# Gated delta rule in a decoder layer: k and q kept in two parts for their products, q's sums of squares by block transposes

## Chip, core and metric

The kernel runs on one core of a Trainium2 chip. A core has a matrix engine (TensorE, here PE; PEld is its weight load), a vector engine (DVE), a scalar engine (ACT), GpSimd (POOL) and a sync engine (SP), each with its own instruction queue that it works through in order; they meet at semaphores. The metric is the device time of one execution in microseconds (us), lower is better.

## What is computed

One layer of a hybrid decoder for 256 tokens and a width of 2048, in float32. After an RMS norm one projection gives q, k, v, z, two small gates, a pooling input and two channel gates. q and k (16 heads of 128) go through a causal convolution of 4 taps and SiLU, are scaled to unit length, and enter a gated delta rule in chunks. What the change touches is this:

```python
qkv = silu(causal_dwconv(concatenate([q, k, v]), conv_qkv_w))
q = l2norm(q) * HEAD_DIM ** -0.5          # l2norm: x * rsqrt(sum(x*x) + EPS)
k = l2norm(k)
lmat = where(strict, einsum('nid,njd->nij', k * beta, k) * decay, 0)
u, w = triangular_solve(lmat + eye, [v * beta, k * beta * exp(g)])
attn_intra = einsum('nid,njd->nij', q, k) * decay
...
o = rmsnorm(o, gdn_norm_w) * silu(z)
```

The mixer's output is merged with a causal pooling branch, projected and added to x; then follow a gated MLP (width 5632) with a convolution of 3 taps and a final norm. Each output must match the float32 reference closely, so that plain reduced-precision products aren't enough.

## The kernel before

Each large GEMM is split: a weight tile `raw` of 256 rows by 512 columns (a chunk) is cast by ACT into a high part `whi` in the format float32r (L131), and DVE makes the low part `wlo` = raw - whi (L139). The activations are held in two such parts as well. `gemm_a` (L156 on) then makes three products a step, high by high, low by high and high by low (L169 to L171), with 512 columns each; a chunk has 12 of them. `weights()` keeps the parts two chunks ahead (`AHEAD = 2`) in three buffers each. `gemm_b` (L193, L194), for the FFN, makes a product of 512 and one of 256 columns a step.

The mixer runs in four groups of four heads (loop at L790). A group's GEMMs are, in order, k, q, v, pooling input, a gate, the pooling weights, z and a gate. A result is scaled out of PSUM by ACT into the one buffer `ev` (`evict`, L526). `conv_silu` (L566) turns it with PE, makes the four taps on ACT and DVE (L577, L580), the tanh on ACT (L583), and writes the SiLU to one half of the tile `kq` (L584); it is called when the next GEMM starts its second chunk (the list `later`). v goes to DRAM (`vrow`) and comes back as shifted copies `mv` (L550), which DVE weighs and adds (L557, L558).

The rest of the delta rule is the generator `gdn` (L586): `side()` in `gemm_a` advances it by one step after each half chunk, from v's GEMM on. Its steps are: decay factors `dec0`, `dec1`; for each head two full float32 products of k with [k q] (L631, L633) into two PSUM tiles; from their diagonal the sums of squares of k (L636); the scaled and decayed tiles `ga0`, `ga1` (L646, L650); diagonal blocks sent through DRAM to a layout (`lb`) in which DVE solves eight problems at once (L676, L678); the inverse T put together from blocks (L697 to L739); products with v (`w1`, `w2`, L745 to L757); the output products `po` (L763 to L766); the squares of q on ACT (L760) and their sums as eight full float32 products of a 128x128 block of squares with a column of ones (L771); and the output's norm (L772 to L786). After its last GEMM a group drains what is left of the generator (`gated`).

The order of each engine's queue isn't written out by hand, except for the first GEMM: the framework plans it at build time from the order of the code and a simulated timeline (`schedule_with_timeline_sim=True`), and sets the semaphores. Tiles of the same tag share its buffers (`bufs`, 1 in this pool unless stated), and a new tile of a tag waits until all that used the older one are done.

Of the kernel before, what the change touches and what calls it, by code (L numbers as in the profile page):

```python
# [13 lines left out]
P = 128  # L14
S = 256
# [18 lines left out]
def kernel(  # L34
# [36 lines left out]
    def pg(shape=(P, 512)):  # L71
        return psg.tile(list(shape), F32, tag="g", name=nm("psg"))
# [133 lines left out]
    def turned(src):  # L206

        out = []
        for f2 in range(2):
            pt = pg([P, 2, S])  # L210
            for ff in range(2):
                f = 2 * f2 + ff
                for t in range(2):
                    nc.tensor.transpose(pt[:, ff, t * P : (t + 1) * P], src[:, t, f * P : (f + 1) * P], ident)
            out.append(pt)
        return out
# [23 lines left out]
    mix = tc.tile_pool(name="mix", bufs=1)  # L240
    mp = mix.__enter__()

    nmrows = mp.tile([KD, P], F32, tag="w1", name="nmrows")
    nc.scalar.dma_start(nmrows, norm_mix_w[0].rearrange("(r p) -> r p", p=P))
    x0 = []
    for c in range(4):
# [174 lines left out]
    nc.vector.tensor_tensor(id2, ident[:64, 0:32], ident[:64, 32:64], op=ALU.add)  # L421


    pba = pg([P, 2, S])
    for c in range(2):
        hi, lo = weights()
        for kk in range(8):
            k = 8 * c + kk
            mm(pba, hi[:, kk, :], xhl[:, k], start=(k == 0), stop=(k == KD - 1))
    bat = mp.tile([64, 2, S], F32, tag="u", name="bat")  # L430
    nc.vector.tensor_copy(bat, pba[:64])
    pbt = pg([P, 2, 32])
    for t in range(2):
# [131 lines left out]

    def conv_silu(e, kind, g, dst):  # L566

        pts = turned(e)
        y = mp.tile([P, 4, S], F32, tag="cy", bufs=2, name=nm("cy"))
        for f in range(4):  # L570
            r = kind * 16 + 4 * g + f
            gs = pts[f // 2][:, f % 2, :]

            def w(j):
                return cqw[:, j * 48 + r : j * 48 + r + 1]

            nc.scalar.activation(y[:, f, :], gs, AF.Copy, scale=w(3))  # L577
            for j in (2, 1, 0):
                s = 3 - j
                nc.vector.scalar_tensor_tensor(y[:, f, s:], gs[:, : S - s], w(j), y[:, f, s:],  # L580
                                               op0=ALU.mult, op1=ALU.add)
        th = mp.tile([P, 4, S], F32, tag="th", name=nm("th"))
        nc.scalar.activation(th, y, AF.Tanh)  # L583
        nc.vector.scalar_tensor_tensor(dst, th, 1.0, y, op0=ALU.add, op1=ALU.mult)  # L584

    def gdn(g, kq, vt, conv, res):  # L586

        ga0 = mp.tile([P, 4, 512], F32, tag="ga0", name=nm("ga0"))
        ga1 = mp.tile([P, 4, 256], F32, tag="ga1", name=nm("ga1"))
# [2 lines left out]
        sj = mp.tile([P, 2, 4], F32, tag="sj", name=nm("sj"))  # L592
        dec0 = mp.tile([P, 4, S], F32, tag="dec0", name=nm("dec0"))
        dec1 = mp.tile([P, 4, P], F32, tag="dec1", name=nm("dec1"))
        for hp in range(2):

            h0 = 2 * hp
            rx = []
            for part, gp in (("h", ghi.bitcast(F32)), ("l", glo)):
                r0 = mp.tile([P, 2, P], F32R, tag="r0" + part, name=nm("r0"))  # L600
                r1 = mp.tile([P, 2, P], F32R, tag="r1" + part, name=nm("r1"))
                for i in range(2):
                    hh = 4 * g + h0 + i
                    nc.vector.tensor_scalar(r0[:, i], tri, gp[:, 0, hh : hh + 1], None, op0=ALU.mult)
                    nc.vector.tensor_scalar(r1[:, i], tri, gp[:, 1, hh : hh + 1], None, op0=ALU.mult)
                rx.append((r0, r1))
            yield
            pd0 = pg([P, 2, P])
            pdx = pg([P, 2, P])
            pd1 = pg([P, 2, P])  # L610
            for n, (r0, r1) in enumerate(rx):
                mm(pd0, lowr, r0, start=(n == 0), stop=(n == 1))
                mm(pd1, lowr, r1, start=(n == 0), stop=(n == 1))
            for n, (r0, r1) in enumerate(rx):
                mm(pdx, onesr, r1, start=(n == 0), stop=(n == 1))
            nc.scalar.activation(dec0[:, h0 : h0 + 2, 0:P], pd0, AF.Exp)
            nc.scalar.activation(dec1[:, h0 : h0 + 2, :], pd1, AF.Exp)
            for i in range(2):
                hh = 4 * g + h0 + i
                nc.scalar.activation(dec0[:, h0 + i, P:S], pdx[:, i, :], AF.Exp, bias=tail[:, hh : hh + 1])  # L620
            for d in (dec0[:, h0 : h0 + 2, 0:P], dec1[:, h0 : h0 + 2, :]):
                nc.gpsimd.affine_select(d, d, pattern=[[0, 2], [1, P]], compare_op=ALU.is_ge, fill=0.0, base=0,
                                        channel_multiplier=-1)
            yield
        for hp in range(2):
# [2 lines left out]
            grams = []  # L628
            for h in (h0, h0 + 1):
                pg0 = pg()  # L630
                mm(pg0, kq[:, h, 0, 0:P], kq[:, h, :, :], start=True, stop=True)  # L631
                pg1 = pg([P, 2, P])
                mm(pg1, kq[:, h, 0, P:S], kq[:, h, :, P:S], start=True, stop=True)  # L633
                jk = mp.tile([P, P], F32, tag="jk", name=nm("jk"))
                for t, src in ((0, pg0[:, 0:P]), (1, pg1[:, 0, :])):
                    nc.vector.tensor_tensor_reduce(jk, src, ident, scale=1.0, scalar=0.0, op0=ALU.mult,  # L636
                                                   op1=ALU.add, accum_out=ssk[:, t, h : h + 1])
                grams.append((pg0, pg1))
                yield
# [50 lines left out]
        for h in range(4):  # L690
            for t in range(2):
                nc.scalar.activation(vt[:, t, h, :], vt[:, t, h, :], AF.Copy, scale=nk[:, t, h : h + 1])
        for _ in range(WAIT - 3):
            yield
        for r in range(NR):
            rs = slice(B0 * r, B0 * (r + 1))
            nc.vector.transpose(Ta[rs, :, rs], TTa[rs, :, rs])  # L697
# [40 lines left out]
                mm(px[lo, t, i, :], U[hp][up, t, i, :], TT[hp][up, t, i, up], start=True, stop=True)  # L738
            nc.vector.tensor_scalar(TT[hp][lo, :, :, up], px[lo], -1.0, None, op0=ALU.mult)  # L739
        yield  # L740
        w1 = mp.tile([P, 4, P], F32, tag="w1", name=nm("w1"))
        w2 = mp.tile([P, 4, P], F32, tag="w2", name=nm("w2"))
        pw = pg([P, 4, P])
        for h in range(4):
            mm(pw[:, h, :], TT[h // 2][:, 0, h % 2, :], vt[:, 0, h, :], start=True, stop=True)  # L745
# [9 lines left out]
            mm(pw[:, h, :], TT[h // 2][:, 1, h % 2, :], vt[:, 1, h, :], start=True, stop=True)  # L755
        nc.scalar.copy(w2, pw)
        yield  # L757

        q2 = kq[:, :, 1, :]
        nc.scalar.activation(q2, q2, AF.Square)  # L760
        po = [pg([P, 4, P]) for t in range(2)]
        for h in range(4):
            mm(po[0][:, h, :], ga0[:, h, 256:384], w1[:, h, :], start=True, stop=True)  # L763
# [1 line left out]
            mm(po[1][:, h, :], ga0[:, h, 384:512], w1[:, h, :], start=True, stop=False)  # L765
            mm(po[1][:, h, :], ga1[:, h, P : 2 * P], w2[:, h, :], start=False, stop=True)  # L766
        yield
        pn = pg([P, 2, 4])
        for t in range(2):
            for h in range(4):  # L770
                mm(pn[:, t, h : h + 1], q2[:, h, t * P : (t + 1) * P], ones[:, 0:1], start=True, stop=True)  # L771
        ro = mp.tile([P, 2, 4], F32, tag="ro", name=nm("ro"))  # L772
        so = mp.tile([P, 2, 4], F32, tag="so", name=nm("so"))
        for t in range(2):
# [1 line left out]
            nc.scalar.activation(o2, po[t], AF.Square, scale=float(P) ** -0.5)  # L776
            nc.vector.tensor_reduce(so[:, t, :], o2, axis=mybir.AxisListType.X, op=ALU.add)
        yield
        nc.vector.tensor_scalar(ro, pn, EPS * P, EPS * EPS * P, op0=ALU.mult, op1=ALU.add)
        nc.vector.tensor_tensor(ro, ro, so, op=ALU.add)  # L780
        nc.gpsimd.tensor_tensor(ro, ro, epsx[:, 0:1].unsqueeze(2).to_broadcast([P, 2, 4]), op=ALU.pow)
        for t in range(2):
# [5 lines left out]
        res.append(on)  # L788

    for g in range(4):  # L790
        kq = mp.tile([P, 4, 2, S], F32, tag="kq", bufs=1, name=nm("kq"))
        for kind, dst in ((1, kq[:, :, 0, :]), (0, kq[:, :, 1, :])):
            ps = ps_k0 if kind == 1 and g == 0 else gemm_a(xh, xl, KD)
            e = evict(ps)
            later.append(lambda e=e, kind=kind, g=g, dst=dst: conv_silu(e, kind, g, dst))
# [1 line left out]
        vt = mp.tile([P, 2, 4, P], F32, tag="vt", name=nm("vt"))  # L797
        vt2 = vt.rearrange("p t h d -> p t (h d)")
        res = []
        later.append(lambda g=g, kq=kq, vt=vt, res=res: side_work.__setitem__(0, gdn(g, kq, vt, v_conv(g, vt), res)))  # L800
        v_taps(g)
        e = evict(gemm_a(xh, xl, KD), rsh)
        nc.sync.dma_start(vrow[g, SH : SH + S, :].rearrange("(t p) d -> p t d", p=P), e)
# [239 lines left out]
```

## Time and profile before

| what | value |
|---|---|
| median of 3 runs | 1576.41 us (1576.08 to 1577.27) |
| the profiled execution's own time | 1577.52 us |
| its span | 1575.6 us |
| mean granted PE clock | 0.999 |
| bytes moved by DMA | 304 MB, mean 193 GB/s |
| mixer's four groups | from some 40 to 780 us |

The profile shows one execution. A row with "x8" stands for eight instructions merged in order of time; times in it are start, length. Lengths of PE's products overlap, so that their cost is read from start to start. A full float32 product shows as two records. In rows of groups the columns after the bar are busy time and mean length in ns, then the engine's idle time before them and what ended it.

### The profile page before, as it was taken

To read this page: it belongs to the slowest core of one execution; us is meant where nothing else is said; L and a number is where in the kernel's file an instruction comes from. 1 tells how busy PE (TensorE), PEld (TensorE's weight loads), DVE (VectorE), ACT (ScalarE), POOL (GpSimd) and SP (SyncE) were. 2 spreads that over 40 slices of the span, in tenths; PEclk is the share of its full clock that TensorE was granted. 3 is DMA by queue.
4 is the path that set the end of the run, shared out by engine and by line. 5 is a ranking of instruction groups with operands and counts; after the bars stand their busy time and mean duration, and the time that the engine had idled before them with its cause. 6 is when DMAs were issued, how large, how long until landed. Compare 5 with 4: busy or idle time off the path is not lost.

```text
span 1575.6 us, 21329 instructions
## 1 busy us (share of the span) xinstructions
PE 1563.7 (99%) x8086; PEld 1315.0 (83%) x8086; DVE 1067.5 (68%) x1623; ACT 745.3 (47%) x954; POOL 45.0 (3%) x69
## 2 busy tenths in 40 slices
PE   9999999999999999999999999999999999999997
PEld 8878888788878888788888888888888888888886
DVE  6897758785698757795556667766766667444444
ACT  6554435544545445444454544444444445334443
POOL 3010000000000000000000000000000000000000
PEclk9999999999999999999999999999999999999999
DMA  7676656775767757675566666666666666656662
GB/s 255 214 230 188 187 160 206 199 217 171 181 208 202 201 147 201 203 208 174 196 193 185 188 187 187 188 188 189 186 194 190 187 189 210 200 191 208 206 217 91
DMA packets 167924, 304.22 MB, mean 193 GB/s; under 512 B 19186, under 2 KB 22274, under 8 KB 167694
## 3 DMA queue, kind: packets, MB, share of 16 engines
q1 hardware_dynamic: 164800, 297.84, 63.3%
q10 hardware_dynamic: 3022, 5.03, 1.0%
q8 instruction: 63, 1.03, 0.3%
q14 instruction: 39, 0.32, 0.1%
HBM read 297.56 MB, written 5.27 MB: 192 GB/s over the span
## 4 chain that ended last, share of the span: by engine, by line
PE 97%; issue 1%; DMA 1%; DVE 1%; ACT 0%; POOLq 0%; POOL 0%; SPq 0%; DVEq 0%
PE psm L171 14%; PE psm L170 14%; PE psm L169 14%; PE psm L193 10%; PE psg L193 10%; PE psg L194 5%; PE psm L194 5%; PE psg L956 2%; PE psg L958 2%; PE psg L957 2%; PE psm L958 2%; PE psm L957 2%; PE psm L956 2%; PE psm L296 1%; PE psg L631 1%
## 5 line engine op out<-in xcount | busy, mean ns | idle before, releaser
L139 DVE TENSOR_TENSOR wlo<-raw,whi 128x1024 fp32r<-128x1024 f32 x524 | 640.1, 1223 | 399.9 <-ACT whi L131 388.4
L131 ACT CAST whi<-raw 128x1024 fp32r<-128x1024 f32 x526 | 553.3, 1053 | 717.4 <-PE psm L170 314.0
L171 PE MATMUL psm<-wlo,xhl 128*128 128x512 f32 x864 | 339.6, 393 | 1.5 <-DVE wlo L139 1.5
L169 PE MATMUL psm<-whi,xhl 128*128 128x512 f32 x864 | 339.0, 392 | 0.0
L170 PE MATMUL psm<-whi,xhl 128*128 128x512 f32 x864 | 338.5, 392 | 0.0
L193 PE MATMUL psm<-fhl,whi 128*128 128x512 f32 x704 | 246.2, 396 | 0.0
L193 PE MATMUL psg<-fhl,whi 128*128 128x512 f32 x704 | 238.0, 394 | 0.0
L194 PE MATMUL psm<-fhl,wlo 128*128 128x256 f32 x704 | 194.4, 279 | 0.0
L171 PEld LDWEIGHTS psm<-wlo,xhl 128*128 128x128 f32 x864 | 162.3, 188 | 35.6 <-DVE wlo L139 2.9
L170 PEld LDWEIGHTS psm<-whi,xhl 128*128 128x128 f32 x864 | 162.3, 188 | 33.5
L169 PEld LDWEIGHTS psm<-whi,xhl 128*128 128x128 f32 x864 | 162.3, 188 | 32.9 <-issue 0.2
L194 PE MATMUL psg<-fhl,wlo 128*128 128x256 f32 x704 | 178.7, 279 | 0.0
L193 PEld LDWEIGHTS psm<-fhl,whi 128*128 128x128 f32 x704 | 131.4, 188 | 30.5
L193 PEld LDWEIGHTS psg<-fhl,whi 128*128 128x128 f32 x704 | 129.2, 188 | 24.2
L194 PEld LDWEIGHTS psg<-fhl,wlo 128*128 128x128 f32 x704 | 132.5, 188 | 6.9
L194 PEld LDWEIGHTS psm<-fhl,wlo 128*128 128x128 f32 x704 | 132.5, 188 | 1.1
L956 PE MATMUL psg<-whi,hhi 128*128 128x512 f32 x168 | 65.5, 390 | 0.0
L957 PE MATMUL psg<-whi,hlo 128*128 128x512 f32 x168 | 65.4, 389 | 0.0
L956 PE MATMUL psm<-whi,hhi 128*128 128x512 f32 x168 | 65.4, 389 | 0.0
L957 PE MATMUL psm<-whi,hlo 128*128 128x512 f32 x168 | 65.4, 389 | 0.0
L958 PE MATMUL psm<-wlo,hhi 128*128 128x512 f32 x168 | 65.4, 389 | 0.0
L958 PE MATMUL psg<-wlo,hhi 128*128 128x512 f32 x168 | 59.0, 389 | 0.0
(257 smaller groups left out, 1518.2 us busy)
## 6 DMA issues: line engine op xcount, KB each, us to landing
raw<-in_w_in_dram SPq DMA_DIRECT2D x226, 512.0 KB, 4.3
raw<-in_w_up_dram SPq DMA_DIRECT2D x176, 512.0 KB, 4.5
raw<-in_w_down_dram SPq DMA_DIRECT2D x88, 512.0 KB, 4.1
raw<-in_w_out_dram SPq DMA_DIRECT2D x32, 512.0 KB, 3.8
mv<-vrow SPq DMA_DIRECT2D x12, 512.0 KB, 5.2
taps<-in_conv_qkv_w_dram SPq DMA_DIRECT2D x16, 256.0 KB, 5.6
raw<-in_pool_w_dram SPq DMA_DIRECT2D x8, 512.0 KB, 6.4
x<-in_x_dram SPq DMA_DIRECT2D x4, 512.0 KB, 8.3
```

The costliest lines, as they stand in the source:

```text
L131: nc.scalar.copy(hi, raw)
L139: nc.vector.tensor_tensor(lo, raw, hi.bitcast(F32), op=ALU.subtract)
L169: mm(ps[:, t, :], lh(k, t), hi[:, kk, :], start=(k == 0), stop=False)
L170: mm(ps[:, t, :], ll(k, t), hi[:, kk, :], start=False, stop=False)
L171: mm(ps[:, t, :], lh(k, t), lo[:, kk, :], start=False, stop=(k == nk - 1))
L193: mm(ps[f], hi[:, kk, fs], rhl(k), start=(k == 0), stop=False, skip_group_check=True)
L194: mm(ps[f][:, 1, :], lo[:, kk, fs], rhl(k)[:, 0, :], start=False, stop=(k == nk - 1), skip_group_check=True)
L296: mm(ps_k0[:, t, :], part(k, t), w[:, kk, :], start=(k == 0 and w is hi and part is xh), stop=(k == KD - 1 and w is lo))
L631: mm(pg0, kq[:, h, 0, 0:P], kq[:, h, :, :], start=True, stop=True)
L956: mm(acc[c][t], lh(k, t), hi[:, kk, :], start=(k == 0), stop=False)
L957: mm(acc[c][t], ll(k, t), hi[:, kk, :], start=False, stop=False)
L958: mm(acc[c][t], lh(k, t), lo[:, kk, :], start=False, stop=(k == KF - 1))
```

## The change

k and q are kept as two tiles, `kqh` (float32r) and `kql` (float32r, the exact difference), where one float32 tile `kq` was. `conv_silu` writes the SiLU in place, ACT copies it to the high part, and DVE subtracts that for the low part. For each head three products (high by high, low by high, high by low) of 512 and of 256 columns add up in the same two PSUM tiles.

For q, ACT squares the SiLU in place right there. The first step of the generator transposes the squares in blocks of 32x32 on DVE into `qx`, a tile with the tag `ev`; the second sums groups of 32 neighbours into `qp` (128x32). At the end one full float32 product of `qp` with a 0/1 matrix `sel` sums over the blocks of 32 partitions, in place of the eight products with ones, and four small steps on 32 partitions each read its result where one step on 128 did. The generator has one yield more. `w1`, `w2` and two tiles of the start take other tags.

```diff
-    nmrows = mp.tile([KD, P], F32, tag="w1", name="nmrows")
+    nmrows = mp.tile([KD, P], F32, tag="ga0", name="nmrows")
...
+    sel = mp.tile([P, 4, 32], F32, name="sel")
+    nc.vector.tensor_reduce(sel[:, 0, :], ident.rearrange("p (b i) -> p i b", b=4), axis=mybir.AxisListType.X,
+                            op=ALU.add)
+    nc.vector.tensor_copy(sel[:, 1:4, :], sel[:, 0:1, :].to_broadcast([P, 3, 32]))
...
-    bat = mp.tile([64, 2, S], F32, tag="u", name="bat")
+    bat = mp.tile([64, 2, S], F32, tag="ga1", name="bat")
...
-        nc.vector.scalar_tensor_tensor(dst, th, 1.0, y, op0=ALU.add, op1=ALU.mult)
-
-    def gdn(g, kq, vt, conv, res):
+        nc.vector.scalar_tensor_tensor(y, th, 1.0, y, op0=ALU.add, op1=ALU.mult)
+        hi, lo = dst
+        nc.scalar.copy(hi, y)
+        nc.vector.tensor_tensor(lo, y, hi.bitcast(F32), op=ALU.subtract)
+        if kind == 0:
+            nc.scalar.activation(y, y, AF.Square)
+            squares.append(y)
+
+    squares = []
+
+    def gdn(g, kqh, kql, vt, conv, res):
...
+        qx = mp.tile([P, 4, S], F32, tag="ev", name=nm("qx"))
+        nc.vector.transpose(qx, squares.pop())
+        yield
+        qp = mp.tile([P, 32], F32, tag="qp", name=nm("qp"))
+        nc.vector.tensor_reduce(qp, qx.rearrange("p h (c j) -> p (h c) j", j=32), axis=mybir.AxisListType.X,
+                                op=ALU.add)
...
-                mm(pg0, kq[:, h, 0, 0:P], kq[:, h, :, :], start=True, stop=True)
                 pg1 = pg([P, 2, P])
-                mm(pg1, kq[:, h, 0, P:S], kq[:, h, :, P:S], start=True, stop=True)
+                for n, (a, b) in enumerate(((kqh, kqh), (kql, kqh), (kqh, kql))):
+                    mm(pg0, a[:, h, 0, 0:P], b[:, h, :, :], start=(n == 0), stop=(n == 2))
+                    mm(pg1, a[:, h, 0, P:S], b[:, h, :, P:S], start=(n == 0), stop=(n == 2))
...
-        for _ in range(WAIT - 3):
-            yield
+        yield
+        yield
...
-        w1 = mp.tile([P, 4, P], F32, tag="w1", name=nm("w1"))
-        w2 = mp.tile([P, 4, P], F32, tag="w2", name=nm("w2"))
+        w1 = mp.tile([P, 4, P], F32, tag="kql", name=nm("w1"))
+        w2 = mp.tile([P, 4, P], F32, tag="kqh", name=nm("w2"))
...
-        q2 = kq[:, :, 1, :]
-        nc.scalar.activation(q2, q2, AF.Square)
...
-        pn = pg([P, 2, 4])
-        for t in range(2):
-            for h in range(4):
-                mm(pn[:, t, h : h + 1], q2[:, h, t * P : (t + 1) * P], ones[:, 0:1], start=True, stop=True)
+        pn = pg([P, 4, 2, 4])
+        mm(pn.rearrange("p h t c -> p (h t c)"), sel.rearrange("p b i -> p (b i)"), qp, start=True, stop=True)
...
-        nc.vector.tensor_scalar(ro, pn, EPS * P, EPS * EPS * P, op0=ALU.mult, op1=ALU.add)
+        for c in range(4):
+            pr = slice(32 * c, 32 * c + 32)
+            nc.vector.tensor_scalar(ro[pr], pn[pr, :, :, c].rearrange("p h t -> p t h"), EPS * P, EPS * EPS * P,
+                                    op0=ALU.mult, op1=ALU.add)
...
-        kq = mp.tile([P, 4, 2, S], F32, tag="kq", bufs=1, name=nm("kq"))
-        for kind, dst in ((1, kq[:, :, 0, :]), (0, kq[:, :, 1, :])):
+        kqh = mp.tile([P, 4, 2, S], F32R, tag="kqh", name=nm("kqh"))
+        kql = mp.tile([P, 4, 2, S], F32R, tag="kql", name=nm("kql"))
+        for kind, n in ((1, 0), (0, 1)):
+            dst = (kqh[:, :, n, :], kql[:, :, n, :])
```

More of the change, by code (lines that the diff above doesn't have):

```diff
@@ L799 @@
         res = []
[L800 removed]
+        later.append(lambda g=g, kqh=kqh, kql=kql, vt=vt, res=res: side_work.__setitem__(
+            0, gdn(g, kqh, kql, vt, v_conv(g, vt), res)))
         v_taps(g)
```

## Prediction

> **What bounds the kernel now.** I read the page's busy times first, then the waits of PE, then PE's instructions in order of time around the lines that change.
>
> ```profile
> span 1575.6 us, 21329 instructions
> ...
> PE 1563.7 (99%) x8086; PEld 1315.0 (83%) x8086; DVE 1067.5 (68%) x1623; ACT 745.3 (47%) x954; POOL 45.0 (3%) x69
> ...
> PEclk9999999999999999999999999999999999999999
> ...
> PE 97%; issue 1%; DMA 1%; DVE 1%; ACT 0%; POOLq 0%; POOL 0%; SPq 0%; DVEq 0%
> ```
>
> PE is busy for 99% of the span at the full granted clock, and 97% of the chain that ended last is PE. So a product taken off PE should shorten the time by what it costs there, unless PE then waits for something. The waits of PE show how near that is:
>
> ```profile
> PE psm L171 <- DVE wlo L139: 1.5, 3, 0.7
> PE psm L233 <- POOL ones L220: 1.0, 1, 1.0
> PE psg L263 <- DVE nmw L302: 0.5, 1, 0.5
> PE psm L296 <- ACT whi L131: 0.5, 1, 0.5
> ```
>
> Only 1.5 us in three places are waits for the low parts of the weights, which DVE makes. The other three rows lie in the start-up. PE has nearly nothing to gain from shorter waits, and everything from fewer or shorter products; what can be lost is that DVE or ACT come late with the next weights.
>
> **The products of k and q (L631, L633).** Today each head has one full-precision product of 512 columns and one of 256, each shown as two records (x2). Two heads in a row, with the GEMM's products before and behind them:
>
> ```profile
> 94.77 0.39 PE L170 MATMUL psm<-whi,xhl 128*128 128x512 f32 x1
> 95.00 1.02 PE L631 MATMUL psg<-kq 128*128 128x512 f32 x2
> ...
> 97.39 0.58 PE L171 MATMUL psm<-wlo,xhl 128*128 128x512 f32 x1
> 97.81 0.39 PE L169 MATMUL psm<-whi,xhl 128*128 128x512 f32 x1
> ```
>
> The durations overlap, so I count from start to start. A GEMM product of 512 columns follows the one before after 0.227 us. From 94.77 to 97.81 are 3.04 us; without the heads it would be two such steps, 0.454. Two heads cost 2.59 us, one 1.29.
>
> The new form is three pairs of a 512- and a 256-column product in the split format, each with weights of its own. The FFN's GEMM runs just this pattern:
>
> ```profile
> 1000.00 0.39 PE L193 MATMUL psg<-fhl,whi 128*128 128x512 f32 x1
> 1000.23 0.27 PE L194 MATMUL psg<-fhl,wlo 128*128 128x256 f32 x1
> 1000.35 0.40 PE L193 MATMUL psg<-fhl,whi 128*128 128x512 f32 x1
> ...
> 1003.12 0.40 PE L193 MATMUL psg<-fhl,whi 128*128 128x512 f32 x1
> ```
>
> ```profile
> L194 PEld LDWEIGHTS psm<-fhl,wlo 128*128 128x128 f32 x704 | 132.5, 188 | 1.1
> ```
>
> Nine pairs take 3.12 us, one 0.347. Three pairs are 1.04 us, so a head gains 0.25 and the 16 heads 4.0 us. Bounds: if the short product cost as much as its weight load is long (0.19, the row of L194's loads), a head would take 3 x (0.227 + 0.19) = 1.25 and all gain 0.6; if no format change beside the heads saves another 0.09 per pair of heads (the step after a full-precision run, below), 0.7 more, 4.7. I take 4.0, because the FFN rows are the same shapes in the same order.
>
> The Trainium skill, "FP8 and Floating Point Precision", section "TensorE Precision Notes", says that true FP32 takes four passes through the array; three products of one pass each would then cost three quarters, 0.97 us a head, and the gain would be an estimated 5.2 us. The row of 512 columns here, 0.86 us between the starts of L631 and L633 against 0.227, is 3.8 passes. My sum stays with 4.0.
>
> **The sums of squares of q (L771).** Sixteen records a group go, two take their place:
>
> ```profile
> 221.64 1.84 PE L771 MATMUL psg<-ones,kq 128*128 128x1 f32 x16
> 223.34 0.48 PE L171 MATMUL psm<-wlo,xhl 128*128 128x512 f32 x1
> ```
>
> ```profile
> 213.50 1.05 PE L750 MATMUL psg<-w,ga 128*128 128x128 f32 x8
> 214.31 0.47 PE L169 MATMUL psm<-whi,xhl 128*128 128x512 f32 x1
> 214.62 0.39 PE L170 MATMUL psm<-whi,xhl 128*128 128x512 f32 x1
> ```
>
> From 221.64 to 223.34 are 1.70 us. The one new product has a full 128x128 load and 32 columns; the nearest are L750's eight records, which take 0.81 us and stretch the next step from 0.227 to 0.31, that is 0.10 a record and 0.09 once. Two records are 0.21 us if they stand beside other full-precision products, 0.30 alone. The gain is 1.4 to 1.5 us a group; I take 1.48, or 5.9 us in four groups (bounds 5.6 and 6.0). PE's sum: 4.0 + 5.9 = 9.9 us less (bounds 6.2 and 10.7).
>
> **What DVE and ACT get for it.** The nearest rows:
>
> ```profile
> L139 DVE TENSOR_TENSOR wlo<-raw,whi 128x1024 fp32r<-128x1024 f32 x524 | 640.1, 1223 | 399.9 <-ACT whi L131 388.4 <-PE psg L214 5.9 <-PE psg L821 2.9
> ...
> L697 DVE STREAM_TRANSPOSE T<-TT 32x256 f32<-32x256 f32 x16 | 7.0, 436 | 2.7 <-DMA TT<-tbd 2.3
> ...
> L777 DVE TENSOR_REDUCE so<-o 128x4 f32<-128x512 f32 x8 | 5.5, 686 | 14.3 <-ACT o L776 14.3
> ...
> L723 DVE STREAM_TRANSPOSE TT<-T 32x128 f32<-32x128 f32 x16 | 4.9, 303 | 0.5
> ```
>
> ```profile
> L131 ACT CAST whi<-raw 128x1024 fp32r<-128x1024 f32 x526 | 553.3, 1053 | 717.4 <-PE psm L170 314.0
> ```
>
> Per group DVE gets two subtractions of 1024 columns (k and q, 1.22 each as L139), one block transpose of 1024 columns (128 more columns cost 0.133 us between L723 and L697, so 0.436 + 6 x 0.133 = 1.23; between 0.44, if length cost nothing more, and 1.74, four times L697), one sum over 1024 columns (1.22 to 1.37, twice L777 at most), and three more small steps on 32 rows (some 0.2 each, below L723). That is 5.4 us a group, 22 in all. ACT gets two casts (1.05 each); the square moves from behind the last product of the heads to the q part, at the same length. The selection matrix is two short DVE steps once, in the start-up, where the other constants are made; uncovered it would cost 0.6 us at most. No DMA is added. The tiles that change their buffer's name at the start are read once and long free. The additional yield puts the steps of a group half a chunk (1.36 us, six products) later against the GEMM; by the code a group's generator then has 47 steps and the GEMMs of its group call it 82 times, so this costs nothing by itself.
>
> Is there room for 5.4 us? DVE, from the first convolution of each group to shortly before its triangular solve:
>
> ```profile
> 60.00:136.00 76.00, 76.00 (x352) 62.20 (x351) 62.86 (x121) 40.92 (x60) 6.91 (x6) 1.00 0.68 204
> 236.00:311.00 75.00, 74.63 (x348) 60.96 (x346) 61.03 (x110) 42.23 (x62) 5.72 (x6) 1.00 0.71 206
> 418.00:490.00 72.00, 72.00 (x330) 58.90 (x328) 58.98 (x105) 39.70 (x58) 4.60 (x6) 1.00 0.75 214
> 600.00:662.00 62.00, 61.18 (x272) 48.98 (x271) 50.56 (x86) 34.00 (x51) 5.27 (x6) 1.00 0.66 194
> ```
>
> The columns are length, then busy time of PE, weight loads, DVE, ACT. DVE is idle for 13.1, 14.0, 13.0 and 11.4 us of these stretches (length less busy), more than twice what is added. But up to 5 us of that is a wait in its queue that extra work may not fill, since what stands behind it waits too:
>
> ```profile
> 308.78 0.42 DVE L676 TENSOR_TENSOR tmp<-lb,tb 128x248 f32<-128x248 f32 x1 [4.99 <-DMA lb<-cdd]
> ```
>
> Behind this step stands the next weight subtraction, and PE waits for that one at 311 us. The order of the queues is planned at build time from a simulated timeline: if the gates and Gram tiles come later in the plan, so does this step, and more weight subtractions go in front. PE therefore loses what plan and chip differ by, not the length of the added work. That difference costs 1.5 us today; I allow as much again. The bounds of this term are 0 (all in DVE's idle time) and 22 us (all on PE's path).
>
> Sum against the profiled execution's own time, 1577.5 us (span 1575.6): 1577.5 - 9.9 + 1.5 = 1569.1. That execution stands 1.1 above the median of the runs, 1576.4, so I forecast **1568**. A measurement here can tell about 0.2% from no change: below 1573.3 is faster, above 1579.6 slower.
>
> **Rivals.** First, the gain of the heads is given back. PE reaches the waits at L676 1.0 us a group sooner, finds DVE no earlier, and stands: 4.0 us return, 1572. For it speaks that PE already waits there; against it, that the gain of L771 comes later, where DVE is not full, and that PE's three waits are short.
>
> Second, DVE's crowded stretch gives all of it back. If half of the 5.4 us of each group delays the Gram tiles and the solve's data with them, the step at L676 comes 2.7 us later against the same weights: 4 x 2.7 = 10.8 in place of the 1.5, 1577.3. For it speaks that DVE is full just before; against it, the plan that moves the weights in front, and the 11 to 14 us idle.
>
> Third, slower: the turned squares share the one buffer "ev" with the evicted GEMM results. So v's eviction on ACT must wait until q's squares are summed, and behind it in ACT's queue wait the high parts of the weights; its copy in DRAM and the shifted v tiles come later too, for which DVE waits in order. Today v's eviction stands like this against the last step of q:
>
> ```profile
> 86.78 1.26 ACT L526 ACTIVATE ev<-psm,rsh 128x512 f32<-128x512 f32 x2
> ...
> 268.94 1.26 ACT L526 ACTIVATE ev<-psm,rsh 128x512 f32<-128x512 f32 x2
> ...
> 450.46 1.26 ACT L526 ACTIVATE ev<-psm,rsh 128x512 f32<-128x512 f32 x2
> ...
> 634.08 1.25 ACT L526 ACTIVATE ev<-psm,rsh 128x512 f32<-128x512 f32 x2
> ```
>
> ```profile
> 90.16 1.21 DVE L584 SCALAR_TENSOR_TENSOR kq<-th,cy 128x1024 f32<-128x1024 f32 x1
> ...
> 264.21 1.23 DVE L584 SCALAR_TENSOR_TENSOR kq<-th,cy 128x1024 f32<-128x1024 f32 x1
> ...
> 444.43 1.22 DVE L584 SCALAR_TENSOR_TENSOR kq<-th,cy 128x1024 f32<-128x1024 f32 x1
> ...
> 624.16 1.22 DVE L584 SCALAR_TENSOR_TENSOR kq<-th,cy 128x1024 f32<-128x1024 f32 x1
> ```
>
> After L584 come a cast and a square on ACT (2.1), transpose and sum on DVE (2.45) and two weight subtractions between them (2.45), 7.0 us. The sums are ready at 98.4, 272.4, 452.7 and 632.4, so v's evictions come 11.6, 3.5 and 2.2 us late, the last one not at all. The weights are made two chunks ahead, 2 x 12 products of 0.227, or 5.4 us. If the first delay counts beyond that lead (6.2) and the others in full, since DVE already stands at the shifted v tiles, 11.9 us return: 1577.5 - 9.9 + 1.5 + 11.9, less 1.1, is 1580. It decides once the planned place of v's eviction is before the sums are ready on the chip. Against it: the plan knows the buffer and can put weights ahead of the eviction.
>
> Fourth, the change does not do what it says: the short products cost their loads, and PE gains 0.6 in place of 4.0. Then it is 1571.4. The FFN rows speak against it.
>
> **How the numbers follow.** The forecast has 0.45, the first rival 0.20, the second 0.15, the slower one 0.17, the fourth 0.03. Faster: 0.45, 0.03, most of the first (0.17) and a little of the second (0.02), 0.67. Slower: most of the third, 0.15. Within 0.2%: the rest, 0.18. The forecast's own range is 1565.5 to 1571: the upper bound of PE's gain with nothing returned gives 1565.7, and with the middle gain 4.5 us returned 1571. The whole range, from 1565 to 1580, takes in the first two rivals and the third up to its price; what is left out is above it.
>
> **What would show it.** Right: six records a head at L631 and L633's successors, pairs 0.35 us apart; two records of the one product per group; PE busy about 10 us less; PE's waits for the weights' low parts below some 3 us. Wrong: PE idle in pieces of 2 us and more behind the solve's first step (second rival), or ACT standing at v's eviction with the weights late behind it (third).

## The result and the profile after

| | before | changed |
|---|---|---|
| time, median of 6 runs, us | 1576.26 (1576.05 to 1577.27) | 1584.09 (1583.63 to 1584.67) |
| profiled execution: its own time, span, us | 1577.5, 1575.6 | 1584.12, 1582.4 |
| mean granted clock of TensorE | 0.999 | 0.994 |

The ratio is 1.005 (95% interval 1.0039 to 1.006): the change makes the kernel 0.5% slower. 1568 was forecast, with 1565 to 1580 as the range. The span grew by 6.8 us, although less work is on PE. The page of the changed kernel, its span, busy times, granted clock by slices and the chain by engine:

```profile
span 1582.4 us, 21321 instructions
...
PE 1559.8 (99%) x8062; PEld 1315.6 (83%) x8062; DVE 1087.2 (69%) x1653; ACT 752.6 (48%) x962; POOL 51.6 (3%) x69
...
PEclk9999999999999999999899999999999999999999
...
PE 96%; DVE 1%; issue 1%; DMA 1%; ACT 1%; POOL 0%; ACTq 0%; SPq 0%; POOLq 0%; DVEq 0%
```

PE was busy for all but 11.9 us of the span before (1575.6 less 1563.7) and is now idle for 22.6. One slice, the twentieth (752 to 791 us), has a lower clock, which also lengthens what PE counts as busy. The waits of PE in the changed kernel (waiting line, what it waited for: us in total, times, the longest):

```profile
PE psg L214 <- DVE sz L876: 7.7, 1, 7.7
PE psm L169 <- ACT phi L848: 2.4, 3, 1.0
PE psm L169 <- ACT ev L532: 2.1, 1, 2.1
...
PE psg L778 <- DVE vt L774: 0.8, 1, 0.8
```

None of these four was there before, and the waits for the low parts of the weights are gone. The longest is L214, PE's turn of `sz`, the merged result of a group (`mixed`), and it waits only once, at the end of the last group.

**The gain on PE is there.** The changed kernel's timeline of PE, at the heads of the third group and at the new product of the last one:

```profile
464.06 0.40 PE L655 MATMUL psg<-kqh 128*128 128x512 f32 x1
...
464.42 0.39 PE L655 MATMUL psg<-kqh,kql 128*128 128x512 f32 x1
...
465.11 0.39 PE L655 MATMUL psg<-kqh,kql 128*128 128x512 f32 x1
...
770.98 0.31 PE L789 MATMUL psg<-qp,sel 128*128 128x32 f32 x2
771.12 0.47 PE L786 MATMUL psg<-w,ga 128*128 128x128 f32 x2
771.43 0.39 PE L785 MATMUL psg<-w,ga 128*128 128x128 f32 x2
771.65 0.39 PE L786 MATMUL psg<-w,ga 128*128 128x128 f32 x2
```

A pair takes 0.36 us at its first step, and from 464.42 to 465.11 two take 0.69, 0.345 each: the 0.347 that the FFN's rows had given. The one product for the sums of squares takes 0.14 us (770.98 to 771.12) and the step behind it 0.31 in place of 0.22, 0.23 us together; 0.21 to 0.30 was allowed.

**Where it is given back.** Both traces have all 1024 records of L169, so the same number in the order is the same product of the GEMMs, and its start tells how far PE has come. Before, in PE's timeline, records 377, 618 and 1001 (in the solves of the second and third group, and behind the last group):

```profile
330.04 0.39 PE L169 MATMUL psm<-whi,xhl 128*128 128x512 f32 x1
...
517.20 0.39 PE L169 MATMUL psm<-whi,xhl 128*128 128x512 f32 x1
...
817.02 0.39 PE L169 MATMUL psm<-whi,mhi 128*128 128x512 f32 x1
```

The same three in the changed kernel's timeline:

```profile
326.60 0.39 PE L169 MATMUL psm<-whi,xhl 128*128 128x512 f32 x1
...
516.26 0.39 PE L169 MATMUL psm<-whi,xhl 128*128 128x512 f32 x1
...
823.78 0.39 PE L169 MATMUL psm<-whi,mhi 128*128 128x512 f32 x1
```

In the second group PE is 3.44 us ahead, close to the 3.48 that the prediction's sum gives for that place: 4 heads of the first group (1.0), its sums (1.48), 4 heads of the second (1.0). In the third it should be 1.48 + 1.0 more ahead, 5.9, and is 0.94: 5.0 us lost. Behind the last group it should be 9.9 ahead, by the prediction's sum, and is 6.76 behind: 16.7 us lost in all, 5.0 in the third group and 11.7 after it.

The third group's loss, in the changed kernel's timeline of PE:

```profile
470.70 0.50 PE L169 MATMUL psm<-whi,xhl 128*128 128x512 f32 x1 [2.08 <-ACT ev L532]
...
471.71 0.63 PE L169 MATMUL psm<-whi,xhl 128*128 128x512 f32 x1
...
474.68 0.39 PE L170 MATMUL psm<-whi,xhl 128*128 128x512 f32 x1
...
499.12 0.50 PE L169 MATMUL psm<-whi,phi 128*128 128x512 f32 x1 [0.72 <-ACT phi L848]
```

PE waits 2.08 us for v's eviction, and soon after that its products follow one another in 0.43 us in place of 0.227, until 474.68. The seven steps from 471.71 cost 1.4 us (2.97 less 7 x 0.227), and pooled tiles that come late with v cost another 0.72: 4.2 of the 5.0.

The last group's loss, in the changed kernel's chain of waits (start, length, what ran):

```profile
772.71 0.24 PE psg L786 x2
...
772.97 0.60 ACT o L794
...
774.63 1.65 POOL ro L802
...
779.27 1.24 DVE sz L876
...
780.64 1.94 PE psg L214 x8
782.58 1.04 PE psm L169 x2
783.62 0.43 PE psm L170
```

From the last product of the delta rule to the turn of the merged result there is a chain over ACT, DVE and GpSimd, and PE has nothing beside it: 7.7 us idle, then eight turns in 1.94 us and products at 0.52 and 0.43 a piece. The same stretch of the chain of before:

```profile
756.45 1.68 PE psg L771 x16
758.13 0.34 PE psm L171
...
774.13 0.87 PE psg L214 x8
```

There PE ran 16.0 us of GEMM products (758.13 to 774.13) between the two, and the same chain ended beneath them; the eight turns took 0.87 us. These products are the early pieces of the output projection, which need only the first three groups. In the changed kernel PE had run the last of them at 766.80, ahead of the last products of the delta rule. The last step of the merged result, in DVE's timeline of before, group by group:

```profile
234.15 1.23 DVE L852 TENSOR_TENSOR sz<-sz,yb 128x1024 f32<-128x1024 f32 x1
...
408.05 1.22 DVE L852 TENSOR_TENSOR sz<-sz,yb 128x1024 f32<-128x1024 f32 x1
...
589.09 1.23 DVE L852 TENSOR_TENSOR sz<-sz,yb 128x1024 f32<-128x1024 f32 x1
...
768.81 1.23 DVE L852 TENSOR_TENSOR sz<-sz,yb 128x1024 f32<-128x1024 f32 x1
```

and in that of the changed kernel:

```profile
242.41 1.22 DVE L876 TENSOR_TENSOR sz<-sz,yb 128x1024 f32<-128x1024 f32 x1
...
427.48 1.23 DVE L876 TENSOR_TENSOR sz<-sz,yb 128x1024 f32<-128x1024 f32 x1
...
611.37 1.22 DVE L876 TENSOR_TENSOR sz<-sz,yb 128x1024 f32<-128x1024 f32 x1
...
779.27 1.22 DVE L876 TENSOR_TENSOR sz<-sz,yb 128x1024 f32<-128x1024 f32 x1
```

Every group ends its delta rule later than before, by 8.3, 19.4, 22.3 and 10.5 us. Before, the last one was ready at 770.04 (768.81 and 1.23), and its turn began at 773.97 in PE's timeline (the chain's row, 774.13, counts from the end of the product ahead of it): 3.9 us in hand, a limit that no list of waits shows, because nothing waited. In the other three groups the turn follows its result by the same 3.9 us before, and by 3.6 to 3.9 in the changed kernel; only behind the last group has PE nothing left to run until then.

### The profile page after: what moved, and what is told of

The parts are those of the page before. It is cut to its first block, busy times and chain, and to the rows that moved or that the text cites. A ratio compares the mean times of both kernels' runs of the same rounds, so it can differ in the third digit from the quotient of the medians.

```text
span 1582.4 us, 21321 instructions
## 1 busy us (share of the span) xinstructions
PE 1559.8 (99%) x8062; PEld 1315.6 (83%) x8062; DVE 1087.2 (69%) x1653; ACT 752.6 (48%) x962; POOL 51.6 (3%) x69
## 4 chain that ended last, share of the span: by engine, by line
PE 96%; DVE 1%; issue 1%; DMA 1%; ACT 1%; POOL 0%; ACTq 0%; SPq 0%; POOLq 0%; DVEq 0%
PE psm L169 14%; PE psm L170 14%; PE psm L171 14%; PE psm L193 10%; PE psg L193 10%; PE psg L194 5%; PE psm L194 5%; PE psg L980 2%; PE psg L982 2%; PE psg L981 2%; PE psm L980 2%; PE psm L982 2%; PE psm L981 2%; PE psm L296 1%; PE psg L214 1%
## 5 line engine op out<-in xcount | busy, mean ns | idle before, releaser
L169 PE MATMUL psm<-whi,xhl 128*128 128x512 f32 x864 | 338.6, 392 | 2.1 <-ACT ev L532 2.1
L169 PEld LDWEIGHTS psm<-whi,xhl 128*128 128x128 f32 x864 | 162.7, 188 | 35.3 <-ACT ev L532 2.7
```

Of the source, the lines that this page charges most:

```text
L169: mm(ps[:, t, :], lh(k, t), hi[:, kk, :], start=(k == 0), stop=False)
```

## The experiments

Times are medians; each ratio is to the kernel before on the same chip (1576.08 to 1576.29 in the three sessions), with its 95% interval.

| run | us | ratio | wait of the last turn (L214), us |
|---|---|---|---|
| e1_qx_th | 1588.82 | 1.0078 (1.0063 to 1.0093) | 7.7 |
| e2_sums_alone | 1577.88 | 1.001 (1.0 to 1.002) | 6.4 |
| e3_products_alone | 1582.9 | 1.0041 (1.0026 to 1.0055) | 7.6 |
| e4_tail_cut | 1576.16 | 1.0 (0.9991 to 1.0009) | none |
| e5_before_free | 1570.55 | 0.9965 (0.9952 to 0.9978) | none |
| e6_noyield | 1584.64 | 1.005 (1.0034 to 1.0067) | 7.7 |
| e7_before_late_turn | 1577.26 | 1.0005 (0.9996 to 1.0015) | none |
| e8_after_late_turn | 1573.88 | 0.9984 (0.9975 to 0.9994) | 6.3 |
| e9_last_full | 1567.49 | 0.9945 (0.9933 to 0.9958) | none |
| e10_sums_late_turn | 1571.82 | 0.9973 (0.9962 to 0.9983) | none |
| e11_pool_low | 1573.62 | 0.9985 (0.9976 to 0.9994) | 6.3 |
| e12_late_turn_th | 1575.9 | 0.9998 (0.9989 to 1.0007) | 7.7 |

### First session: v's eviction, or the work itself

**The turned squares in another buffer.** In the changed kernel:

```diff
-        qx = mp.tile([P, 4, S], F32, tag="ev", name=nm("qx"))
+        qx = mp.tile([P, 4, S], F32, tag="th", name=nm("qx"))
```

> The changed kernel with one edit: the transposed squares lie in the buffer of the tanh (tag th), which is free then, and not in that of the evicted GEMM results (ev). Theory A (v's eviction, held up by q's sums through the shared buffer, makes both losses: the stop of the third group and, since the v path is late, the late end of the last group): v's eviction comes within 2 us of its place in the kernel before, both PE waits go, 1566 to 1570 us. Theory B (the added work between q's SiLU and the products delays the delta rule from group to group, whatever the buffer): only the third group's stop goes (2.1 us of wait and the slow clock behind it, 5.0 us in all), the 7.7 us wait before the last group's turn stays, 1577 to 1581 us.

It became slower still, outside both ranges. A new wait of PE:

```profile
PE psg L843 <- DVE ga L669: 7.3, 3, 3.1
```

v's evictions are back near their old times (the first at 87.53, against 86.78 before and 98.05 in the changed kernel), and the wait for `ev` is gone. But the Gram tiles are no earlier: in the last group the final step of L673 starts at 680.56. PE now waits 7.3 us for them, since the pooling needs the buffers that they hold, and 7.7 at the end as before. With v early the delta rule ends no earlier. But with the tanh's buffer held, the heads' products end later too (in the first group the last one starts at 123.66, against 111.46 in the changed kernel), so that this run alone does not say what v's late eviction costs.

**One half of the change at a time.** e2 keeps the one f32 tile of k and q and its full products, and takes the new sums:

```diff
-        nc.vector.scalar_tensor_tensor(y, th, 1.0, y, op0=ALU.add, op1=ALU.mult)
-        hi, lo = dst
-        nc.scalar.copy(hi, y)
-        nc.vector.tensor_tensor(lo, y, hi.bitcast(F32), op=ALU.subtract)
+        nc.vector.scalar_tensor_tensor(dst, th, 1.0, y, op0=ALU.add, op1=ALU.mult)
...
-            nc.scalar.activation(y, y, AF.Square)
+            nc.scalar.activation(y, dst, AF.Square)
...
+                mm(pg0, kq[:, h, 0, 0:P], kq[:, h, :, :], start=True, stop=True)
+                mm(pg1, kq[:, h, 0, P:S], kq[:, h, :, P:S], start=True, stop=True)
```

e3 has the three products, and the sums of squares in the old way, from q's high part alone (as the squares lie in `kql` until then, `w1` and `w2` share the buffer of `kqh`):

```diff
+        q2 = kql[:, :, 1, :].bitcast(F32)
+        nc.scalar.activation(kql[:, :, 1, :], kqh[:, :, 1, :].bitcast(F32), AF.Square)
...
-        mm(pn.rearrange("p h t c -> p (h t c)"), sel.rearrange("p b i -> p (b i)"), qp, start=True, stop=True)
+        for t in range(2):
+            for h in range(4):
+                mm(pn[:, t, h : h + 1], q2[:, h, t * P : (t + 1) * P], ones[:, 0:1], start=True, stop=True)
```

> Only the new sums of squares, in the buffer ev as in the change; k and q stay one float32 tile with one full product each. PE has 5.9 us less than before. Theory A: v's eviction still waits for the sums, the last group still ends late, 1576 to 1583 us. Theory B: without the casts and subtractions of the parts the slide is about half, and the last group's wait is under 3 us, 1570 to 1575 us.

> Only the products in three instructions; the sums of squares as before, by eight full products with ones, with the squares taken from the high part of q alone and rounded (the low part is left out of the sum). PE has 4.0 us less than before. Theory A: nothing holds v's eviction, 1571 to 1574 us. Theory B: the parts still delay the products, the last group's wait stays at 3 us or more, 1576 to 1583 us.

Either half alone brings the bare wait at the end, 6.4 and 7.6 us. The sums alone give back all of their 5.9 us (1.6 above before), the products 4.0 and 6.6 more. The one cause in the half with the parts, which I had expected to show here, isn't there: each half makes the delta rule late by itself. The first group's merged result is ready 4.0 us later than before in e2 and 6.0 in e3 (its last step starts at 238.13 and 240.13, against 234.15). In e3 v's first eviction is at 87.40, near its old 86.78, so the delay there does not need a late v.

**The end of the last group cut.** In the last group alone the merged result leaves out the delta rule's output:

```diff
+            if last:
+                nc.vector.tensor_tensor(sz, yb, sz, op=ALU.mult)
+            else:
                 nc.vector.tensor_tensor(sz, res[0].rearrange("p t h d -> p t (h d)"), sz, op=ALU.mult)
```

> The changed kernel, but the last group's merged rows leave out the delta rule's output (it is computed and not used), so that nothing behind it waits for its end. Both theories: the loss at the end of the last group (7.7 us of wait, 0.8 before it, and the slow clock after) is some 11.5 us and goes, while the third group's stop stays: 1571 to 1575 us. If the loss lay elsewhere (slower products, contention), the time would stay above 1580 us.

8.0 us less than the changed kernel (1584.09 to 1576.16), though 1.2 us above the range expected. So the wait at the end and the slow products behind it are about half of the 16.7 us lost, and the waits for `ev` (2.1) and `phi` (2.7), still there, belong to the rest.

### Second session: is there anything to gain, and does lateness travel

**The gain without the work.** The kernel before, without the squares and sums of q (the norm takes the sums of the output in their place):

```diff
-        q2 = kq[:, :, 1, :]
-        nc.scalar.activation(q2, q2, AF.Square)
...
-        nc.vector.tensor_scalar(ro, pn, EPS * P, EPS * EPS * P, op0=ALU.mult, op1=ALU.add)
+        nc.vector.tensor_scalar(ro, so, EPS * P, EPS * EPS * P, op0=ALU.mult, op1=ALU.add)
```

> The kernel before without the squares of q and their sums: neither the square on ACT nor the eight full products a group run, and nothing takes their place (q's norm is left out of the output's norm). PE has 6.8 us less and no engine has more. Theory C (a second bound: the last group's delta rule ends, in the kernel before, only 4 us ahead of PE's turn of its result, so no more than some 4 us can be gained on PE): 1571 to 1573.5 us, with a new PE wait of 2 us or more before that turn. If PE were the only bound: 1569 to 1570 us and no such wait.

PE's 6.8 us less work become 5.6 us of time, without a wait, so the limit of some 4 us that I had expected did not show. The 3.9 us in hand don't limit the gain as long as the end of the delta rule moves with PE: `sz` ends at 764.3 there, against 770.0 before.

**No yield between transpose and sum.** One `yield` is taken out of the changed kernel.

> The changed kernel without the additional yield, so that the sum of the squares stands in the same step as their transpose and all later steps stand half a chunk (1.36 us) earlier in the code. If the yield sets how late the delta rule ends: 4 x 1.36, some 5 us back, 1577 to 1580 us. Theory C and B (a chain of waits from group to group, which the planned order follows and not the calls): within 2 us of the changed kernel, 1582 to 1586 us.

The same time and the same waits: the additional yield costs nothing, as predicted.

**The turn of the merged result later.** So far it is planned ahead of the next group's turn of k, which follows it at once on PE (in the kernel before at 240.19, behind 239.31). Here it goes behind that group's convolution of k, in the kernel before (e7) and in the changed one (e8):

```diff
+    held = []
...
+            if kind == 1 and held:
+                later.append(held.pop())
...
-            later.append(mixed)
+            held.append(mixed)
```

> The kernel before with the turn of a group's merged result placed after the next group's convolution of k in place of ahead of it (the first three groups; the result isn't needed until the output projection). Theory D (the delta rule's end in one group holds up the next group's k through that turn, so lateness is handed on): k's SiLU in the second group comes 5 us or more sooner, the delta rule ends sooner; PE has no wait to lose there but its 1.5 us, so 1574 to 1576.5 us. If it hands nothing on: no earlier SiLU, 1576 to 1578 us.

> The changed kernel with the same later turn. Theory D: the lateness isn't handed on from group to group, the last group's wait of 7.7 us goes or falls below 3 us, and most of PE's 9.9 us shows: 1567 to 1574 us, faster than both kernels. If the lateness arises in each group anew: 1581 to 1586 us.

In the kernel before it changes nothing in the time, although k of the second group is 11.5 us sooner (its last step at 239.58, against 251.04): PE had next to no wait there to lose (1.5 us in three places). In the changed kernel it brings 10.2 us (1584.09 to 1573.88), with the same instructions, and makes it faster than before. What moved, in three rows of the last group, k's last step on DVE: of before,

```profile
605.98 1.22 DVE L584 SCALAR_TENSOR_TENSOR kq<-th,cy 128x1024 f32<-128x1024 f32 x1
```

of the changed kernel,

```profile
629.97 1.22 DVE L591 SCALAR_TENSOR_TENSOR cy<-th,cy 128x1024 f32<-128x1024 f32 x1
```

and of e8:

```profile
600.15 1.22 DVE L591 SCALAR_TENSOR_TENSOR cy<-th,cy 128x1024 f32<-128x1024 f32 x1
```

A late end of one group had held back the start of the next, 24.0 us by the last one; with the turn out of its way k is 5.8 us earlier than before. The distance shows the tie: with the old turn, k's last step starts 16.9 us behind the last step of `sz` of the group ahead in all three later groups of the kernel before, and 18.6 or 18.7 behind it in the changed kernel; in e8 it is 2.3 to 4.7.

PE still waits 6.3 us at the end. But the delta rule is no longer late there; in e8's timeline of DVE its result is where it was before (768.81):

```profile
768.69 1.22 DVE L879 TENSOR_TENSOR sz<-sz,yb 128x1024 f32<-128x1024 f32 x1
```

PE comes to the turn 10.2 us sooner (at 763.8, which is 770.06 less the wait of 6.27, in place of 773.97) and stands for all of that but the 3.9 us that were in hand.

### Third session: what is left in the last group

**No parts in the last group.** e8, but with k and q of the last group in one f32 tile and one full-precision product a head, as before; its sums stay new:

```diff
-        kqh = mp.tile([P, 4, 2, S], F32R, tag="kqh", name=nm("kqh"))
-        kql = mp.tile([P, 4, 2, S], F32R, tag="kql", name=nm("kql"))
+        kqh = mp.tile([P, 4, 2, S], F32R if g < 3 else F32, tag="kqh", name=nm("kqh"))
+        kql = mp.tile([P, 4, 2, S], F32R, tag="kql", name=nm("kql")) if g < 3 else None
...
+                sets = ((kqh, kqh),) if kql is None else ((kqh, kqh), (kql, kqh), (kqh, kql))
```

> The changed kernel with the later turn, and in the last group alone k and q stay one float32 tile with one full product each (its sums of squares stay new). PE gets 1.0 us more. Theory E (with nothing handed on, what is left of the last group's wait, 6.3 us, comes from the casts and subtractions of the parts of that group, which delay its products): the last merged result is ready some 4 us sooner, the wait falls to 1 to 3 us, 1569 to 1572 us. If the wait comes from PE's being ahead alone: it stays at 5 us or more, 1574 to 1575.5 us.

1567.49, the fastest of all: 8.6 us below before (ratio 0.9945) and better than expected. The 1001st product of L169, from its timeline:

```profile
807.37 0.39 PE L169 MATMUL psm<-whi,mhi 128*128 128x512 f32 x1
```

It stands 9.65 us ahead of before there, a little more than the sum without the last group's heads (9.9 less 1.0); the wait of the turn is gone.

**The sums alone with the late turn.** e2 with the edit of e8.

> The new sums of squares alone (full products of one float32 tile), with the later turn. PE has 5.9 us less than before. Theory E: the last group isn't delayed by parts, a wait of 3 us or less is left, 1570 to 1573 us. If the sums alone hold the chain up as much as parts and sums together: a wait of 5 us or more, 1574.5 to 1577 us.

1571.82, no wait at the end: 4.3 us less than before, of the 5.9 that its sums take off PE. The transpose and the sum can be hidden once their lateness isn't handed on.

**The low parts on another engine.** e8 with the two subtractions of a group on GpSimd:

```diff
-        nc.vector.tensor_tensor(lo, y, hi.bitcast(F32), op=ALU.subtract)
+        nc.gpsimd.tensor_tensor(lo, y, hi.bitcast(F32), op=ALU.subtract)
```

> The changed kernel with the later turn, and the low parts of k and q subtracted on GpSimd in place of DVE, which has 2.4 us less a group for it. If DVE's load sets the delay (theory L): the delta rule ends earlier, 1569 to 1572 us. If it is the length of the chain from SiLU to product (theory E), or if GpSimd's own step is longer than DVE's: no earlier products, the last wait stays at 5 us or more, 1574 to 1580 us.

The same time as e8, and the same wait of 6.3, though DVE has two subtractions of 1.22 us a group less to do. A step of GpSimd, and the pair of DVE's steps that met it:

```profile
269.83 2.45 POOL L594 TENSOR_TENSOR kql<-cy,kqh 128x1024 fp32r<-128x1024 f32 x1 [0.90 <-ACT kqh L593]
```

```profile
269.93 2.79 DVE L627 TENSOR_SCALAR r<-tri,ghi 128x128 fp32r<-128x128 f32 x2
```

The step is 1.2 us longer on GpSimd, and DVE's pair takes 2.79 us where it takes 0.48 in e8. DVE's busy time in the whole span is only 1.7 us below e8's (1085.3 to 1083.6), though the eight subtractions were 9.7 us of it. So the run hardly relieves DVE, and leaves open whether DVE's load sets the delay.

**The late turn, the other buffer and no yield together.** e8 with the edits of e1 and e6.

> The changed kernel with the later turn, the transposed squares in the tanh's buffer and no additional yield, so that v's eviction waits for nothing of q. If v's path is what is late in the last group (theory V): v's eviction 6 us or more sooner than with the later turn alone, the wait falls below 3 us, 1569 to 1572 us. If it is the products' chain (theory E): v earlier, the merged result not, 1573 to 1578 us.

1575.9, 2.0 us slower than e8, with 7.7 us of wait at the end. v's eviction in the last group is 5 us earlier (622 against 627), and nothing is gained by it: with the tanh's buffer held, the heads' products end later (in the last group the last one starts at 658.36, against 639.38 in e8).

## Why the prediction was wrong

**The chosen value of the returned time is the step that failed.** The prediction's sum was 1577.5 - 9.9 + 1.5; the measured one is 1577.5 - 9.9 + 16.7 = 1584.3, against 1584.1. The 1.5 came from "PE therefore loses what plan and chip differ by, not the length of added work". It was read from DVE's idle time and from PE's waits, that is, as a question of room. But the added steps stand in DVE's and ACT's queues ahead of the delta rule's own or among them, and the delta rule is a chain up to the turn of its result. In the first group, where nothing is handed on yet, the heads' products end even sooner than before (the last record starts at 111.46, against 116.29). DVE's last Gram tile is late all the same. Before:

```profile
119.50 0.47 DVE L650 SCALAR_TENSOR_TENSOR ga<-psg,sj,dec 128x256 f32<-128x256 f32 x1
```

and in the changed kernel, 6.0 us later:

```profile
125.50 0.47 DVE L673 SCALAR_TENSOR_TENSOR ga<-psg,sj,dec 128x256 f32<-128x256 f32 x1
```

At its end in the last group this chain had 3.9 us in hand before PE would wait. The upper bound that the prediction itself gave for this term, 22 us, lies above the 16.7; the range stopped at the third rival's price.

**The gain on PE was right.** In the second group 3.48 us were due and 3.44 came; e5 and e9 show that PE turns such a gain into time when nothing at the end is late.

**The yield.** e6 shows the yield free. The argument beside it was too wide, though: 47 steps in 82 calls means only that the generator gets to its end before the group does. It says nothing of how much GEMM is left for PE behind it, which is what the last group lacks.

**First rival, the data's wait.** Not seen: no wait of PE stands behind L676's successor, L699, and the 3.44 us were kept in the second group.

**Second rival, DVE's crowded stretch.** Its sign, PE idle in pieces of 2 us and more, came, but not where it was put: not behind the solve's first step, but at v's eviction and at the end. Whether DVE's load is behind the delay is not shown, since e11 hardly relieved DVE. DVE's busy time in the whole span grew by 19.7 us (1067.5 to 1087.2), near the 22 that were added, so the sizes were right.

**Third rival, v's eviction: the place was right, the price not shown.** v's evictions in ACT's timeline of the changed kernel:

```profile
98.05 1.27 ACT L532 ACTIVATE ev<-psm,rsh 128x512 f32<-128x512 f32 x2 [2.42 <-DVE qp L615]
...
284.42 1.26 ACT L532 ACTIVATE ev<-psm,rsh 128x512 f32<-128x512 f32 x2
...
469.39 1.26 ACT L532 ACTIVATE ev<-psm,rsh 128x512 f32<-128x512 f32 x2
...
650.95 1.27 ACT L532 ACTIVATE ev<-psm,rsh 128x512 f32<-128x512 f32 x2 [2.42 <-DVE qp L615]
```

The rows of the first and the last group show the wait for q's sums. All four come 11.3, 15.5, 18.9 and 16.9 us later than before, where 11.6, 3.5, 2.2 and nothing were forecast. The first group's delay is right to 0.3 us. The later ones are late because k and q of these groups already are (q's last step by 9.8, 14.5 and 17.0 us), which the rival had not seen. When they are freed, in e1, the 2.1 us of the third group go, but the time gets worse (that the tanh's buffer, now held, is why is not shown); and in e3, with v's first eviction near its old place, the first group still ends 6.0 us late. How much of the delay comes by way of v is not shown.

**What the runs put in its place.** Shown: the delta rule ends later in each group; the turn of its result, planned ahead of the next group's k, hands the delay on (e8 takes 10.2 us back by moving that turn alone in the code); in the last group the work that could cover it has run out, so the chain behind the delta rule lies bare (e4, 8.0 us back). With the later turn that chain ends where it did before, and still PE's gain becomes time only as far as its end comes sooner too (e8, with a wait of 6.3; e9, the wait gone and 6.4 us less than e8). Open: why the merged result of the first group is already 8.3 us late for steps that the prediction adds up to 7.0, weights between them included, and why the parts of the last group make its end 5.8 us later (the last step of `sz` starts at 762.89 in e9 and at 768.69 in e8) when cast and subtraction of q are 2.3. The plan is made anew for each kernel, and no run here held it fixed; that the planned order is the cause there would be argued, not shown. A buffer of their own for the turned squares wasn't tried either: e1 and e12 let them wait for another tile's.

## What to carry to other kernels

An engine at 99% is no licence to count each product taken off it as time: ask for each chain that ends in a wait of that engine how far ahead of that engine it now ends, here 3.9 us at one place, and whether the new steps lie in that chain. Where stages repeat, look at the order of the hand-over: a late end that is planned ahead of the next start is handed on from stage to stage, and it is cheap to move it. The last stage has least to hide its tail behind; it may deserve the old form, even where the new one is better everywhere else.

## What the runs showed of the hardware

**A short stand of PE can be followed by slow steps.** Soon after the wait of 2.08 us that ends at 470.70 PE's steps are 0.43 us, until 474.68, and behind the 7.7 us at the end they are slow as well. The windows view of the changed kernel (length; busy time of PE, weight loads, DVE, ACT and GpSimd; granted clock; DMA share; GB/s):

```profile
468.00:476.00 8.00, 5.92 (x20) 4.46 (x19) 5.82 (x17) 2.80 (x4) 1.84 (x1) 0.79 0.61 193
...
772.00:786.00 14.00, 6.29 (x27) 5.14 (x26) 7.03 (x12) 1.77 (x3) 1.64 (x1) 0.63 0.20 61
786.00:800.00 14.00, 14.00 (x68) 11.63 (x67) 8.80 (x10) 9.31 (x17) 0.00 (x0) 1.00 0.76 245
```

The granted clock is 0.79 and 0.63 there and 1.00 right behind the second, so the stand of 2.08 us cost 1.4 us more at least. It need not: e6 has the same wait of 2.08 us and a clock of 0.79 in the window 468 to 476, but e4, again with a wait of 2.08 us, has 1.00 in that window and no slow step behind it. In e1 a stand of 2.8 us has none either (1.00 in 494 to 502). What decides it no run here shows. The Trainium skill, "TensorE: Matmul & The Clock Gate", Part 1, says that the clock falls to half after an idle window of about 3.4 us and recovers after as long a busy one. The slow steps, 0.43 for 0.227, are near its half, and their length, some 3 us, near its window; but in the changed kernel and e6 2.08 us of idle time were enough.

**GpSimd takes twice DVE's time for the same subtraction**, 2.4 to 2.5 us in six of e11's eight steps (3.0 in the other two) against 1.22 on DVE, for 1024 columns. The Trainium skill, "GPSIMD Engine Reference", section "Elementwise — side-by-side cycle accounting", gives a ratio of 1.96 for an addition; the 2.0 here agrees.

**Some steps of DVE that met GpSimd's subtraction ended only with it.** In e11 that befell DVE four times beside the eight subtractions. Three steps `r<-tri,ghi` of 128 columns took 2.4 us where the others take 0.3 or 0.4, and each ends within 0.1 us of GpSimd's step; one weight subtraction that began beside it took 3.15 us in place of 1.22. The taps `cy` (L587) beside it kept their 0.47 us.
